# Two decay blocks of a gated recurrence: narrow stationary operands and plain copies in place of full-width products and predicated merges

## The chip, the cores and the metric

The kernel runs on one core of one Trainium2 chip. TensorE (PE) multiplies matrices: it holds a stationary operand, loaded by a weight load (PEld in the profile), and streams a moving operand past it into PSUM. VectorE (DVE), ScalarE (ACT) and GpSimd (POOL) work on tiles in SBUF; SyncE (SP) issues most of the DMA transfers. Each engine executes its own queue in order and waits for others by semaphores. The metric is the time of one execution on the device in microseconds (us), given as the median of several runs.

## The reference, cut to what matters

Two layers, each of a half-step SwiGLU FFN, a mixer and a second half-step FFN, over 512 tokens of width 1024. The mixer has three groups of heads side by side: four of stick-breaking attention (A), four of dilated attention (B) and four of a gated recurrence, HGRN2 (C), with 128 keys and 128 values a head. The change is in the recurrence:

```python
def step(state, xs):
    qb, kb, vb, gb = xs
    diff = gb[:, :, :, None, :] - gb[:, :, None, :, :]
    decay = jnp.where(causal, jnp.exp(jnp.where(causal, diff, 0.0)), 0.0)
    scores = jnp.einsum('bhtd,bhsd,bhtsd->bhts', qb, kb, decay)
    o = jnp.einsum('bhts,bhsv->bhtv', scores, vb) + jnp.einsum('bhtd,bhdv->bhtv', qb * jnp.exp(gb), state)
```

Here `gb` is the running sum of the logarithm of the forget gate. A score of a query t and an earlier key s is a sum over the 128 channels of q, k and a decay that depends on t, s and the channel.

## The kernel before

All of it works on tiles with 128 partitions. Projections and FFNs split both operands into a high and a low fp32r part and take three products (`triple`); the names in the profile are `wt` for the split weights, `h` and `hs` for activations, `m` and `a` for the two pools of PSUM banks (two and six), `u` for the general slots of SBUF, `k` for slots of attention keys, `x` for the residual. Nearly every instruction is recorded through a helper and has the line L113.

**The recurrence.** `hgrn(h)` treats one head, with chunks of 128 tokens (four, `NT`) instead of the reference's 64. Within a chunk, scores are built in the tile `st`, keys on partitions and queries along the free axis, by halving: at the level of block m (`LEVELS` = 64, 32, 16, 8, 4, 2, 1) the second half of every stretch of 2m tokens looks at its first half. With the decay measured from the boundary between the halves, one factor belongs to the keys and one to the queries, and a plain matrix product gives the scores.

- `decay` has POOL subtract the boundary's running sum, two operations a level; ACT takes the exponential; DVE multiplies the first halves by k and the second halves by q. The result is the tile `e`.
- `level` multiplies, for each of the four chunks, all 128 tokens of `e` as stationary columns by the 64 tokens of the second halves as moving columns, in fp32: 128 x 64 results, of which only the (first half, second half) pairs of the same stretch count.
- `merge` copies those into `st` under a mask, with one predicated copy on DVE (`copy_predicated`, mask `level_mask`).
- `chain` runs the seven levels of a head in order. Before it, `st` is set to 0 and the diagonal is merged; after it come the state across chunks, the product with the values, a norm and a gate.

**What sets the order.** The program is written out ahead of time by a planner. Pieces of work are generators that yield a `Step` with its engine and the tiles that it needs; `Flow.run` always advances the one that can start earliest by the planner's clocks. `Flow.cost` prices each instruction, and `to_hi` chooses among engines for a copy by the same clocks. So a changed cost or a changed instruction moves other work of the stage. In a mixer the main stream does the projections; four lanes take the tasks `c0,c1,a0,a1,a2,a3,c2,c3,b0,b1,b2,b3` beside it. Heads c0 and c1 run about 440 to 480 us from the start, c2 and c3 in 560 to 632, the dilated heads until about 680. At the end, the main stream's work is the output projection (`out_ac`, tiles `m<-u,wt` of 512 columns), whose last part (`out_b`) has to wait for the dilated heads; `attend` makes a dilated head's output from its weights, which are transposed (`a<-ident,u`), cast on ACT and subtracted on DVE first. The second layer's mixer, about 1476 to 1716 us, repeats this.

Of the kernel before, what the change touches and what calls it, by code (L numbers as in the profile page):

```python
# [17 lines left out]
P = 128  # L18
# [6 lines left out]
NT = S // P  # L25
# [198 lines left out]
class Flow:  # L224
# [15 lines left out]
    def cost(self, eng, op, out, ins):  # L240
        n = out.free_size()
        if eng == "PE":
            if op == "transpose":
                return 0.109
            if ins[0].dtype == F32R:
                return max(0.112, 0.0133 + n / 2400.0)
            return 2 * max(0.112, n / 1200.0)
        psum = any(a.space == bass.MemoryType.PSUM for a in [out, *ins])
        column = any(a.free_size() == 1 for a in ins)
        if eng == "ACT":  # L250
            return 0.18 + n * 0.00085 + 0.05 * column
        if eng == "DVE":
            if op == "tensor_reduce":
                n = ins[0].free_size()
            fast = op in ("tensor_copy", "tensor_scalar") and not psum
            return (0.2 if fast else 0.15) + n * (0.00053 if fast else 0.00108)
        if eng == "POOL":
            return 0.1 + n * (0.0011 if op == "tensor_scalar" else 0.0022)
        return 0.0
# [88 lines left out]
def trunk(ctx, tc, x, c, w_mod, b_mod, f1g, f1u, f1d, w_in, w_out, qng, kng, hng, lbl, f2g, f2u, f2d, cf, out):  # L348
    nc = tc.nc
    F = Flow()  # L350
    V, A, G, T, Q, Q2 = (Engine(F, e, n) for e, n in (
        (nc.vector, "DVE"), (nc.scalar, "ACT"), (nc.gpsimd, "POOL"), (nc.tensor, "PE"), (nc.sync, "SP"),
        (nc.gpsimd, "SP")))

    def space(name, bufs, **kw):
        return ctx.enter_context(tc.tile_pool(name=name, bufs=bufs, **kw))
# [9 lines left out]
    B = Pool(F, space("psa", 6, space=PS), "a", [P, S], 6)  # L366
# [555 lines left out]
    def next_weight():  # L922
        if not weights:
            yield lambda: bool(weights)
        return weights.popleft()
# [407 lines left out]
    def to_hi(out_, in_, engines=("ACT", "DVE", "POOL")):  # L1333
        n = out_.free_size()
        psum = in_.space == PS
        c = {"ACT": 0.1 + n * 0.00083, "DVE": 0.07 + n * (0.00104 if psum else 0.00052), "POOL": 0.1 + n * 0.0011}
        es = [e for e in engines if not (psum and e == "POOL")]
        e = min(es, key=lambda z: max(F.clk[z], max(F.ready.get(n, 0.0) for n in F.keys(in_))) + c[z])
        if e == "ACT":
            A.copy(out_, in_)  # L1340
        elif e == "DVE":
            V.tensor_copy(out_, in_)
        else:
            G.tensor_scalar(out_, in_, 1.0, 0.0, ALU.mult, ALU.add)

    def mixer(phase, l, hs):
# [147 lines left out]
        def blocks(t, m):  # L1494
            return t.rearrange("p (b w) -> p b w", w=2 * m)

        def hgrn(h):
# [8 lines left out]
            st = U.get()  # L1506
# [11 lines left out]
            def level(idx, e):  # L1518

                m = LEVELS[idx]  # L1520
                ps = B.get()
                for t in range(NT):
                    tt = slice(t * P, (t + 1) * P)
                    T.matmul(ps[:, t * 64:(t + 1) * 64].rearrange("p (b w) -> p b w", w=m), e[:, tt],
                             blocks(e[:, tt], m)[:, :, m:], start=True, stop=True)
                return ps

            def merge(idx, ps):
                m = LEVELS[idx]
                mask = level_mask[:, idx * 64:(idx + 1) * 64].rearrange("p (o b w) -> p o b w", o=1, w=m)  # L1530
                V.copy_predicated(
                    st.rearrange("p (t b w) -> p t b w", t=NT, w=2 * m)[:, :, :, m:],
                    mask.to_broadcast([P, NT, 64 // m, m]),
                    ps[:, :256].rearrange("p (t b w) -> p t b w", t=NT, w=m))
                B.put(ps)

            def chain(which):
                for j, idx in enumerate(which):
                    if j == 0:
                        yield Step("POOL", gc, need=((U, 1),))  # L1540
                        decay(idx)
                    if j + 1 < len(which):
                        yield Step("POOL", need=((U, 1),))
                        decay(which[j + 1])
                    e = es[idx]
                    yield Step("ACT", e)
                    A.activation(e, e, AF.Exp)
                    m = LEVELS[idx]
                    eb = blocks(e, m)
                    yield Step("DVE", e)  # L1550
                    V.tensor_mul(eb[:, :, :m], eb[:, :, :m], blocks(k, m)[:, :, :m])
                    V.tensor_mul(eb[:, :, m:], eb[:, :, m:], blocks(q, m)[:, :, m:])
                    yield Step("PE", e, need=((B, 1),))
                    ps = level(idx, e)
                    U.put(e)
                    yield Step("DVE", ps)
                    merge(idx, ps)

            yield Step("PE", k, q, need=((B, 1),))
            ps = B.get()  # L1560
# [58 lines left out]
            o, sq = qe, U.get()  # L1619
# [236 lines left out]
        for name in PROJ.split(",")[2:]:  # L1856
            kind, p = name[0], int(name[1]) if name[1].isdigit() else 0
# [32 lines left out]
        for d in range(0, ND - 2, 2):  # L1890
            w = yield from next_weight()
# [8 lines left out]
        w = yield from next_weight()  # L1900
# [3 lines left out]
        for t, cs in enumerate(HALVES):  # L1904
            for n, d in enumerate(order[t]):
                pool = (M, B)[n % 2]
                yield Step("PE", need=((pool, 1),))
                ps = pool.get()
# [65 lines left out]
```

## Time and profile before

| | |
|---|---|
| runs | 2100.08, 2101.84, 2103.24 us; median 2101.84 |
| profiled execution | 2105.25 us, span of its instructions 2103.5 us |
| mean granted TensorE clock | 0.992 of full speed |
| level matmuls `a<-u` 128x64 | 448 records (224 matmuls in two passes), 56.0 us busy |
| predicated copies of the levels | 56, 28.7 us busy on DVE |
| POOL's operations of 128x256, the levels' 112 subtractions among them | 162, 136.5 us busy |

A row of the timeline gives the start, the length, the engine, the line, the operation, the tiles written and read, the shape, the count of merged instructions, and in brackets the idle time before them with what ended it. A row of a group has the count, the busy time and mean length of one in ns, and the idle time before. The length of a matmul's record reaches past the start of the next one, since they are pipelined; the spacing of starts is what a matmul costs in a stream. An fp32 matmul has two records, an fp32r one a single record.

### The profile page before, as it was taken

The page shows a single profiled execution, that of the slowest core. Times are in us where ns is not written, and L with a number is a line of the kernel's source. Part 1 is how long each engine was busy: PE and PEld are TensorE (multiplying, and loading weights), DVE is VectorE, ACT ScalarE, POOL GpSimd, SP SyncE. Part 2 cuts the span into 40 slices and gives each one's busy share as a digit, 9 for nine tenths or more (in the row PEclk, how much of TensorE's full clock was granted, in tenths as well). Part 3 has the DMA queues.
Part 4 walks back from the last instruction along what each step waited for, and adds up shares of the span by engine and source line. Part 5 has one row for each costly group of instructions (what it writes and reads, how often), then busy time and mean ns, then how long its engine had stood idle before and what let it go on. Part 6 is the DMA issues. An engine that isn't in the chain of part 4 may idle for free.

```text
span 2103.5 us, 31674 instructions
## 1 busy us (share of the span) xinstructions
PE 2055.7 (98%) x12560; PEld 1839.9 (87%) x12560; DVE 1533.8 (73%) x2411; ACT 980.1 (47%) x1628; POOL 192.1 (9%) x236
## 2 busy tenths in 40 slices
PE   7999999999999999999999999999999999999999
PEld 6888888998988987989898898989888888889897
DVE  6887777787688776867686887767876779657463
ACT  5523434556664542534354252436485645335241
POOL 0000000150240100000000000002314101000000
PEclk8999999999999999999999999999999999999999
DMA  9375566211203244354614636442111142533221
GB/s 329 121 232 183 166 200 220 80 42 41 71 31 103 78 144 156 121 181 140 198 53 131 220 121 220 155 146 81 41 40 52 34 134 65 172 109 120 81 81 40
DMA packets 210564, 259.40 MB, mean 123 GB/s; under 512 B 8896, under 2 KB 192084, under 8 KB 210416
## 3 DMA queue, kind: packets, MB, share of 16 engines
q1 hardware_dynamic: 210160, 257.30, 37.9%
q8 instruction: 98, 1.61, 0.3%
q14 instruction: 50, 0.41, 0.1%
q0 software_dynamic: 256, 0.08, 0.0%
HBM read 255.25 MB, written 2.10 MB: 122 GB/s over the span
## 4 chain that ended last, share of the span: by engine, by line
PE 91%; DVE 5%; ACT 1%; DMA 1%; issue 1%; SPq 0%; ACTq 0%; DVEq 0%
PE m L113 56%; PE a L113 35%; DVE u L113 2%; DVE wt L113 1%; ACT u L113 1%; DMA u<-in_w_mod_dram 1%; DVE h L113 1%; DVE x L113 1%; ACT wt L113 0%; DMA w<-in_ffn_w_gate_dram 0%; DVE acc L113 0%; DVE k L113 0%; DVE c L113 0%; SPq L113 0%; ACT h L113 0%
## 5 line engine op out<-in xcount | busy, mean ns | idle before, releaser
L113 PE MATMUL m<-h,wt 128*128 128x512 f32 (+1 forms) x2940 | 579.6, 348 | 12.8 <-DVE h L113 5.5
L113 DVE TENSOR_TENSOR wt<-w,wt 128x1024 fp32r<-128x1024 f32 (+1 forms) x440 | 504.9, 1153 | 112.2 <-ACT wt L113 101.3
L113 PE MATMUL m<-u,wt 128*128 128x512 f32 (+1 forms) x2712 | 574.5, 370 | 10.0 <-DVE x L113 5.1
L113 ACT CAST wt<-w 128x1024 fp32r<-128x1024 f32 (+1 forms) x440 | 423.8, 980 | 338.5 <-PE m L113 147.7
L113 PEld LDWEIGHTS m<-u,wt 128*128 128x128 f32 x2712 | 469.8, 190 | 94.2 <-DVE x L113 8.3
L113 PEld LDWEIGHTS m<-h,wt 128*128 128x128 f32 x2940 | 465.4, 190 | 80.0 <-DVE h L113 9.1
L113 PE MATMUL a<-h,wt 128*128 128x256 f32 (+1 forms) x2172 | 372.1, 327 | 0.0
L113 PEld LDWEIGHTS a<-h,wt 128*128 128x128 f32 x2172 | 325.7, 191 | 33.7
L113 DVE TENSOR_TENSOR u<-u 128x256 f32<-128x256 f32 (+4 forms) x428 | 248.5, 599 | 40.2 <-ACT u L113 33.6
L113 POOL TENSOR_TENSOR u<-u 128x256 f32<-128x256 f32 x162 | 136.5, 863 | 1315.2 <-ACT u L113 1228.1
L113 PE MATMUL a<-hs,wt 128*128 128x256 f32 x1656 | 213.7, 283 | 0.0
L113 PEld LDWEIGHTS a<-hs,wt 128*128 128x128 f32 x1656 | 205.3, 192 | 0.0
L113 DVE SCALAR_TENSOR_TENSOR x<-m,mod,x 128x512 f32<-128x512 f32 (+1 forms) x136 | 90.8, 670 | 123.0 <-PE m L113 122.7
L113 ACT ACTIVATE u<-u 128x512 f32<-128x512 f32 (+2 forms) x264 | 143.2, 568 | 47.7 <-POOL u L113 29.4
L113 DVE SCALAR_TENSOR_TENSOR acc<-w,sc_c,acc 128x1024 f32<-128x1024 f32 x112 | 143.5, 1282 | 2.0
L113 DVE TENSOR_TENSOR w<-w 128x512 f32<-128x512 f32 x184 | 126.9, 690 | 4.7
L113 PEld LDWEIGHTS a<-u 128*128 128x128 f32 x864 | 115.2, 191 | 15.1 <-DVE u L113 3.3
L113 ACT CAST u<-u 128x512 fp32r<-128x512 f32 x98 | 60.7, 620 | 132.0 <-DVE u L113 124.1
L113 PE MATMUL a<-u 128*128 128x64 f32 (+4 forms) x864 | 117.4, 283 | 4.1 <-DVE u L113 3.0
L113 DVE TENSOR_TENSOR u<-u,a 128x256 f32<-128x256 f32 (+1 forms) x88 | 47.9, 546 | 83.3 <-PE a L113 83.3
L113 ACT COPY u<-a 128x256 f32<-128x256 f32 (+2 forms) x131 | 51.5, 393 | 112.1 <-PE a L113 111.2
L113 PE MATMUL m<-wt,h 128*128 128x256 f32 x768 | 100.9, 292 | 2.0 <-DVE u L113 2.0
(145 smaller groups left out, 1423.6 us busy)
## 6 DMA issues: line engine op xcount, KB each, us to landing
w<-in_w_mod_dram SPq DMA_DIRECT2D x128, 512.0 KB, 4.5
w<-in_ffn_w_gate_dram SPq DMA_DIRECT2D x88, 512.0 KB, 4.7
w<-in_ffn_w_up_dram SPq DMA_DIRECT2D x88, 512.0 KB, 4.8
w<-in_ffn_w_down_dram SPq DMA_DIRECT2D x80, 512.0 KB, 4.6
w<-in_w_in_dram SPq DMA_DIRECT2D x56, 512.0 KB, 4.4
u<-in_w_mod_dram SPq DMA_DIRECT2D x32, 256.0 KB, 6.2
w<-in_w_out_dram SPq DMA_DIRECT2D x24, 256.0 KB, 3.3
w<-in_ffn_w_down_dram SPq DMA_DIRECT2D x16, 256.0 KB, 4.8
```

The source lines that it names most:

```text
L113: ins = fn(*args, **kw)
```

## The change

For the blocks of 64 and 32, `level` now makes one matmul for each stretch of 2m tokens, with only the m keys of its first half as stationary columns and the m queries of its second half as moving columns. For block 64 that is one matmul for each chunk, 64 x 64 in place of 128 x 64; for block 32 two for each chunk, 32 x 32. Each result lies on the partitions of its keys. Since all results count, `merge` copies them with `to_hi` (ACT or DVE), one copy for block 64 and two for block 32, instead of one predicated copy each. The planner's price of an fp32 matmul falls with the number of output partitions. The other blocks are as before.

```diff
-            return 2 * max(0.112, n / 1200.0)
+            return 2 * max(0.112 * out.shape[0] / P, n / 1200.0)
...
                 m = LEVELS[idx]
                 ps = B.get()
+                if m >= 32:
+
+                    for t in range(NT):
+                        for b in range(0, P, 2 * m):
+                            o = t * P + b
+                            T.matmul(ps[b:b + m, t * 64 + b // 2:t * 64 + b // 2 + m], e[:, o:o + m],
+                                     e[:, o + m:o + 2 * m], start=True, stop=True)
+                    return ps
...
             def merge(idx, ps):
                 m = LEVELS[idx]
+                if m >= 32:
+                    for b in range(0, P, 2 * m):
+                        r = slice(b, b + m)
+                        to_hi(st[r].rearrange("p (t w) -> p t w", t=NT)[:, :, b + m:b + 2 * m],
+                              ps[r, :256].rearrange("p (t w) -> p t w", t=NT)[:, :, b // 2:b // 2 + m], ("ACT", "DVE"))
+                    B.put(ps)
+                    return
```

In the built program, PE has 32 matmuls of 64x64 and 64 of 32x32 in place of 64 of 128x64. All 24 copies stand on ACT, 8 of 64x4x64 and 16 of 32x4x32; 16 predicated copies are gone from DVE. Six conversions of 128x512 move from ACT and DVE to POOL.

PE at the first levels of the first layer, before (`a<-u` are the levels of heads 0 and 1 in turn, `m<-h,wt` the projections between them):

```order
L113 MATMUL m<-h,wt 128x512 x9
L113 MATMUL a<-u 128x64 x4
L113 MATMUL m<-h,wt 128x512 x3
L113 MATMUL a<-u 128x64 x4
L113 MATMUL m<-h,wt 128x512 x3
L113 MATMUL a<-u 128x64 x4
L113 MATMUL m<-h,wt 128x512 x3
L113 MATMUL a<-u 128x64 x4
```

The same place after the change:

```order
L113 MATMUL m<-h,wt 128x512 x9
L113 MATMUL a<-u 64x64 x4
L113 MATMUL m<-h,wt 128x512 x6
L113 MATMUL a<-u 64x64 x4
L113 MATMUL m<-h,wt 128x512 x6
L113 MATMUL a<-u 32x32 x8
L113 MATMUL m<-h,wt 128x512 x6
L113 MATMUL a<-u 32x32 x8
```

Between two touched levels stand six projection matmuls now instead of three; every touched level has plain matmuls on both sides.

ACT at the same levels, before the change nothing but the exponentials of the levels (`ACTIVATE u<-u 128x512`) and other work; now:

```order
L113 ACTIVATE u<-u 128x512 x2
L113 COPY u<-a 64x4x64
L113 ACTIVATE u<-u 128x512
L113 COPY u<-a 64x4x64
L113 ACTIVATE u<-u 128x512
L113 COPY u<-a 32x4x32 x2
```

The copies that wait for PE stand between the exponentials, and casts of weights follow later in the queue.

PE at the end of the first mixer, before: the transposes of the last dilated head (`a<-ident,u`), its attention (`a<-u` of 512 to 128 columns) and the output projection (`m<-u,wt`):

```order
L113 MATMUL a<-ident,u 128x128 x4
L113 MATMUL m<-u,wt 128x512 x6
L113 MATMUL a<-ident,u 128x128 x2
L113 MATMUL m<-u,wt 128x512 x3
L113 MATMUL a<-ident,u 128x128 x4
L113 MATMUL m<-u,wt 128x512 x12
L113 MATMUL a<-u 128x512 x3
L113 MATMUL a<-u 128x384 x3
```

The same place after the change:

```order
L113 MATMUL a<-k,u 128x128 x3
L113 MATMUL m<-u,wt 128x512 x18
L113 MATMUL a<-ident,u 128x128 x10
L113 MATMUL a<-u 128x512 x3
L113 MATMUL a<-u 128x384 x3
```

No output matmul stands among or behind the transposes any more (21 did), and the attention follows the transposes at once. The second layer has the same rows there. At the start of this part, the first output matmuls follow nine score matmuls (`a<-k,u 128x512 x9`) where six stood before.

## The prediction

> **What bounds the kernel now.** The page comes first: its span, the busy times, and the chain of work that ended last.
>
> ```profile
> span 2103.5 us, 31674 instructions
> PE 2055.7 (98%) x12560; PEld 1839.9 (87%) x12560; DVE 1533.8 (73%) x2411; ACT 980.1 (47%) x1628; POOL 192.1 (9%) x236
> PE 91%; DVE 5%; ACT 1%; DMA 1%; issue 1%; SPq 0%; ACTq 0%; DVEq 0%
> ```
>
> PE (TensorE) is busy for 98% of the span and holds 91% of the chain, so an edit counts by the PE time that it takes away or adds, and by the waits that it opens in front of PE. Since a busy PE is not PE at its peak, I then look at how close its instructions start. The change sits in the two mixers, so the busy times by stage come next (columns: length, then PE, PEld, DVE, ACT, POOL with counts, the granted clock, DMA).
>
> ```profile
> 440.00:480.00 40.00, 39.97 (x262) 35.77 (x262) 33.30 (x61) 18.13 (x34) 18.15 (x24) 1.00 0.09 28
> 560.00:632.00 72.00, 69.11 (x463) 61.40 (x463) 55.05 (x93) 45.10 (x81) 27.22 (x35) 1.00 0.11 34
> 632.00:680.00 48.00, 45.46 (x245) 38.20 (x243) 39.87 (x115) 24.01 (x56) 0.00 (x0) 1.00 0.28 89
> ```
>
> The first stretch holds the levels of heads 0 and 1, the second those of heads 2 and 3, the third the end of the mixer. PE is full in the first and idle for 2.9 and 2.5 us in the others; DVE is at 76 to 83%, ACT at 45 to 63%. What PE waited for from 440 to 700 us (in total, times, longest):
>
> ```profile
> PE m L113 <- DVE u L113: 3.1, 3, 1.2
> PE a L113 <- DVE u L113: 1.5, 1, 1.5
> ```
>
> So most of what PE waits for there is DVE, at the end of the stage and not at the levels.
>
> **A level now.** PE's order of time in the first chain, and a run of seven plain matmuls for their spacing:
>
> ```profile
> 445.48 1.00 PE L113 MATMUL a<-u 128*128 128x64 f32 x8
> 446.29 0.94 PE L113 MATMUL m<-h,wt 128*128 128x512 f32 x3
> 447.07 1.00 PE L113 MATMUL a<-u 128*128 128x64 f32 x8
> 56.47 1.75 PE L113 MATMUL a<-h,wt 128*128 128x512 f32 x7
> L113 PE MATMUL m<-h,wt 128*128 128x512 f32 x1632 | 403.1, 397 | 2.0 <-ACT h L113 1.7 <-DVE h L113 0.3
> ```
>
> A level is four fp32 matmuls, eight records: two passes each, each with a weight load. From level to level it is 1.59 us. The seven matmuls start (1.75 - 0.39) / 6 = 0.227 us apart, so the three between take 0.68, and a level 0.91 us, or 0.114 us a pass. Sixteen levels are touched (two levels, eight heads over both layers): 14.6 us of PE.
>
> **What a narrower pass costs.** No pass of this trace has fewer than 128 stationary columns, so I bound it. Above: the price does not depend on the columns and stays 0.114. Below: the streaming of the moving columns, from an fp32 matmul with 512 of them:
>
> ```profile
> 607.59 1.02 PE L113 MATMUL a<-u,kept 128*128 128x512 f32 x2
> L113 PE MATMUL a<-u,kept 128*128 128x512 f32 x16 | 8.2, 592 | 0.0
> ```
>
> Its two passes start 1.02 - 0.59 = 0.43 us apart, 0.84 ns a column: 0.054 us for 64 columns and 0.027 for 32. Block 64 keeps eight passes: 0.43 to 0.91 us. Block 32 goes from eight to sixteen: 0.43 to 1.82 us. I take 0.057 for both, half the price for half the columns, and no less for a quarter: that is the middle, in ratio, of 0.027 and 0.114. So block 64 has 0.46 us of passes, block 32 has 0.91.
>
> The Trainium skill, "TensorE: Matmul & The Clock Gate", section "LDWEIGHTS (loading the stationary operand)", lets a weight load take its columns divided by 1.2 ns: 107, 53 and 27 ns for 128, 64 and 32. The 0.114 us above agrees with the first; no run here shows the others. By that rule alone, block 32 would stay at its lower bound.
>
> **What a change of array shape costs.** In the built program all matmuls of before have the tile 128x128, but for two transposes of few rows (32x128); the new ones have 128x64 and 128x32. One of the two transposes, of tpar, runs between plain matmuls; the transpose of tb comes from the same helper, with the tile 128x128.
>
> ```profile
> 58.15 0.23 PE L113 MATMUL a<-ident,tpar 14*128 14x14 f32 x1
> 58.31 1.43 PE L113 MATMUL m<-h,wt 128*128 128x512 f32 x5
> 58.15 0.14 PEld L113 LDWEIGHTS a<-ident,tpar 14*128 14x128 f32 x1 [0.35 <-issue]
> 96.04 1.24 PE L113 MATMUL a<-h,wt 128*128 128x256 f32 x9
> 97.12 0.23 PE L113 MATMUL a<-ident,tb 72*128 72x72 f32 x1
> 97.15 0.60 PE L113 MATMUL a<-h,wt 128*128 128x256 f32 x3
> 97.02 0.14 PEld L113 LDWEIGHTS a<-ident,tb 72*128 72x128 f32 x1
> ```
>
> Ahead of tpar the last matmul starts at 57.83 (56.47 + 6 x 0.227), the second one behind it at 58.67 (the end 59.74, less 0.39 and three spacings): 0.84 us, or 0.38 beyond two spacings. For tb the same runs from 97.00 to 97.35: 0.11 beyond two spacings of 0.12. The weight load of tpar came late for "issue", which names no engine. I read the difference, 0.27 us, as the way into another shape and back; the lower bound for columns instead of rows is nothing. All sixteen levels have plain matmuls on both sides, so each pays it: 4.3 us.
>
> The Trainium skill, "TensorEngine Tiling (Array Packing)", section "Key Properties", speaks against the change with the same mechanism: a change of tiling mode drains the array. The late load at 58.15 agrees; without the rule and the row the sum below would be 4.3 us lower.
>
> **Sum on PE.** Block 64: 0.27 + 0.46 - 0.91 = -0.18 us. Block 32: 0.27 + 0.91 - 0.91 = +0.27. A head +0.09, eight heads +0.7 us. Bounds: -7.7 us (no switch, lower prices: 2 x -0.48 x 8) and +11.6 (0.27 + 0.27 + 0.91 = 1.45 a head).
>
> **Merges.** Sixteen predicated copies go from DVE; 24 plain copies come, all on ACT by the new order: 8 of 256 elements and 16 of 128.
>
> ```profile
> L113 DVE COPY_PREDICATED u<-level_mask,a 128x256 f32<-128x256 uint8 x56 | 28.7, 524 | 10.2 <-PE a L113 10.2
> L113 ACT COPY u<-a 128x256 f32<-128x256 f32 x115 | 42.8, 372 | 94.0 <-PE a L113 93.1
> L113 ACT COPY u<-a 128x512 f32<-128x512 f32 x10 | 5.8, 583 | 12.5 <-PE a L113 12.5
> ```
>
> DVE loses 16 x 0.52 = 8.4 us. ACT gains 8 x 0.37 + 16 x 0.27 (the two rows continued to 128 elements) = 7.3 us. Both lie beside PE, so I count nothing. A copy now waits for PE in ACT's queue, with exponentials and weight casts behind it; ACT has at least a third of these stretches free. Were that cover gone, a wait would be about a copy, 0.4 us, a level. On the other side, DVE's relief can at most end PE's waits for it, 4.6 us in this layer. The planner also hands six conversions from ACT and DVE to POOL, which is 9% busy; SP's transfers keep their order.
>
> **The order at the mixer's end.** The planner's new costs move other work. For the last dilated head, the order shows ten transposes in a row and the attention matmuls at once behind them, where twelve matmuls stood between. Before:
>
> ```profile
> 673.39 0.60 PE L113 MATMUL a<-ident,u 128*128 128x128 f32 x4
> 673.75 3.00 PE L113 MATMUL m<-u,wt 128*128 128x512 f32 x12
> 674.03 0.59 ACT L113 CAST u<-a 128x512 fp32r<-128x512 f32 x1 [0.71 <-PE a L113]
> 674.65 0.69 DVE L113 TENSOR_TENSOR u<-a,u 128x512 fp32r<-128x512 f32 x1 [0.87 <-ACT u L113]
> 676.58 2.02 PE L113 MATMUL a<-u 128*128 128x512 f32 x12
> 672.95 0.37 ACT L113 CAST u<-a 128x256 fp32r<-128x256 f32 x1 [1.05 <-PE a L113]
> 634.48 0.96 PE L113 MATMUL m<-u,wt 128*128 128x512 f32 x3 [1.21 <-DVE u L113]
> ```
>
> The twelve covered the cast and the subtraction: the attention at 676.58 waited for nothing. Now the first cast starts 0.64 us after the first transpose, three casts take 0.59 + 0.37 + 0.59, the last subtraction 0.69, with hand-overs 3.0 us; ten transposes (0.11 each, as tb's) take 1.1. PE stands for 1.9 us. Against that, the first output group now follows nine score matmuls instead of six, so 0.7 of the 1.2 us of wait at 634.48 goes. Net 1.2 us a layer, 2.4 us in all; bounds nothing (the work moved ahead fills other waits) and 3.8.
>
> **Total:** +0.7 + 2.4 = +3.1 us. The profiled execution took 2105.25 us (span 2103.5), 3.4 above the median; I put the difference on the median, 2101.84: **2104.9 us**. A measurement of this kernel can tell 0.2%, 4.2 us, from no change.
>
> **Rivals.**
> *A, narrow passes are no cheaper.* PE pays 0.114 for each of block 32's sixteen passes: +11.6 + 2.4 = 2115.9 us. For it: all passes seen, transposes included, start 0.11 us apart or more, as a fixed price would have it; against it: all have 128 columns. It decides early: with the rest as forecast, 0.066 us for block 32's 128 passes makes +4.2.
> *B, no price for the shape.* tpar's gap came from something else, narrow passes stream at their bound, and the end loses nothing: -7.7, 2094.1 us. Against it stands tb, the same helper without the gap.
> *C, the load's columns alone.* Switches at 0.27 and lower bounds for the passes: (0.27 + 0.43 - 0.91) x 2 x 8 = -3.4, with the end's 2.4 a little under before: 2100.8 us. The page's rule for weight loads gives this.
> *D, DVE was the limit.* With 8.4 us off DVE, two thirds of PE's waits for it (4.6 us here, as much taken for the other mixer) go, -6.1, and with them the end's new wait: 0.7 - 6.1 = -5.4, 2096.4 us. Against it: the waits lie behind chains of single operations, not behind a full queue.
>
> **How the numbers follow.** Forecast 0.38, of which 0.14 beyond +4.2; A in all its degrees from 0.066 on 0.22; C 0.20, of which 0.01 beyond -4.2; B 0.14, of which 0.03 within; D 0.06. Faster 0.01 + 0.11 + 0.06 = 0.18; slower 0.14 + 0.22 = 0.36; same 0.46. The range goes over the bounds of the unknown costs, from B to A: 2094 to 2116; the forecast alone has 2102 to 2107.
>
> **What would show it.** Level to level in the new first chain: six matmuls (1.36 us) and 0.73 us for block 64, 1.18 for block 32. Steps between weight loads inside a group give the narrow pass; the time from the last plain matmul to the first narrow load, and back, gives the switch. The twelve attention matmuls behind the ten transposes should carry a wait of about 1.9 us in each layer. The forecast is wrong if block 32 takes much under 0.8 or over 1.4 us, or if PE's waits from 560 to 700 us do not grow.

## The result, and the profile after

| | before | after |
|---|---|---|
| median of the runs | 2101.32 us (4 runs, 2100.08 to 2103.24) | 2123.24 us (4 runs, 2118.61 to 2127.56) |
| ratio to before | | 1.0100, 95% interval 1.0085 to 1.0115 |
| profiled execution | 2105.25 us, span 2103.5 | 2127.56 us, span 2125.8 |

The change makes the kernel slower by 1%, some 22 us by the medians. The four runs after the change fall into two groups, 2118.6 and 2119.4 us and 2127.1 and 2127.6 us, so no run lies at the median, and the profile is of the later group. Span and busy times of the changed kernel:

```profile
span 2125.8 us, 31767 instructions
PE 2062.4 (97%) x12624; PEld 1838.3 (86%) x12624; DVE 1526.7 (72%) x2395; ACT 985.8 (46%) x1646; POOL 200.4 (9%) x242
```

PE is busy for 7 us more, though 64 full-width matmuls became 96 narrower ones, and idle for 16 us more. (The busy time holds matmuls that ran at half clock in this execution; a second profile, of after_again below, with less of that, has PE busy for 2054.3 us.) The touched levels come first. PE's timeline of the first chain, and its weight loads there:

```profile
445.25 0.68 PE L113 MATMUL a<-u 128*64 128x64 f32 x8
445.86 1.66 PE L113 MATMUL m<-h,wt 128*128 128x512 f32 x6
447.45 0.68 PE L113 MATMUL a<-u 128*64 128x64 f32 x8
...
449.66 0.45 PE L113 MATMUL a<-u 128*32 128x32 f32 x16
450.03 1.67 PE L113 MATMUL m<-h,wt 128*128 128x512 f32 x6
451.63 0.45 PE L113 MATMUL a<-u 128*32 128x32 f32 x16
```

```profile
445.25 0.54 PEld L113 LDWEIGHTS a<-u 128*64 128x64 f32 x8 [0.36 <-issue]
...
449.66 0.33 PEld L113 LDWEIGHTS a<-u 128*32 128x32 f32 x16 [0.37 <-issue]
```

Grouped by shape, over the stretch from 440 to 640 us:

```profile
L113 PEld LDWEIGHTS a<-u 128*64 128x64 f32 x32 | 2.2, 137 | 1.4 <-issue 1.4
L113 PEld LDWEIGHTS a<-u 128*32 128x32 f32 x64 | 1.3, 112 | 1.5 <-issue 0.7 <-ACT u L113 0.7
```

Level to level is 2.20 us for block 64 and 1.97 for block 32. Less six matmuls (1.36 us) that leaves **0.84 and 0.61 us a level**, against 0.91 before. One load's length taken off, eight loads of 64 columns start (0.54 - 0.137) / 7 = 0.058 us apart, sixteen of 32 columns (0.33 - 0.112) / 15 = 0.015. Eight passes of 0.058 and sixteen of 0.015 leave 0.38 us a level, the same for both blocks; I put this remainder down to the change of shape. So the levels themselves got cheaper, by 0.07 + 0.30 = 0.37 us a head, 3.0 us in all. The loss lies elsewhere.

What PE waits for in total (times, longest), after and then before:

```profile
PE a L113 <- DVE u L113: 10.3, 4, 3.0
PE m L113 <- DVE k L113: 7.7, 2, 3.8
```

```profile
PE m L113 <- DVE x L113: 7.9, 11, 2.0
PE m L113 <- DVE h L113: 5.5, 13, 1.0
PE m L113 <- DVE u L113: 5.4, 6, 1.2
```

A wait for `k` of 3.8 us in each mixer is new. PE's waits in the first mixer of the changed kernel, from its timeline:

```profile
491.20 11.53 PE L113 MATMUL m<-wt,h 128*128 128x256 f32 x72 [3.84 <-DVE k L113]
...
631.74 1.38 PE L113 MATMUL a<-u 128*128 128x128 f32 x10 [2.95 <-DVE u L113]
...
681.30 1.25 PE L113 MATMUL a<-ident,u 128*128 128x128 f32 x10
683.39 0.50 PE L113 MATMUL a<-u 128*128 128x512 f32 x1 [0.84 <-ACT u L113]
686.08 3.36 PE L113 MATMUL a<-u 128*128 128x512 f32 x11 [2.18 <-DVE u L113]
690.10 2.16 PE L113 MATMUL m<-u,wt 128*128 128x256 f32 x6 [0.67 <-ACT u L113]
```

The first row is where nothing was expected. DVE's queue ahead of it, ACT's cast of the same keys, and then the same subtraction on DVE before:

```profile
483.65 0.75 DVE L113 SCALAR_TENSOR_TENSOR u<-u,par 128x512 f32<-128x512 f32 x1 [5.10 <-ACT u L113]
484.44 0.69 DVE L113 TENSOR_TENSOR u<-u 128x512 f32<-128x512 f32 x1
485.22 0.75 DVE L113 SCALAR_TENSOR_TENSOR u<-u,par 128x512 f32<-128x512 f32 x1
486.01 1.58 DVE L113 TENSOR_TENSOR u<-u 128x512 f32<-128x512 f32 x2
487.51 1.63 DVE L113 TENSOR_TENSOR wt<-w,wt 128x1024 fp32r<-128x1024 f32 x1
489.06 0.68 DVE L113 TENSOR_TENSOR u<-u 128x512 fp32r<-128x512 f32 x1
489.67 1.38 DVE L113 TENSOR_TENSOR k<-m,k 64x512 fp32r<-64x512 f32 x2
```

```profile
485.09 1.17 ACT L113 CAST k<-m 64x512 fp32r<-64x512 f32 x2
```

```profile
486.22 1.39 DVE L113 TENSOR_TENSOR k<-m,k 64x512 fp32r<-64x512 f32 x2 [1.07 <-ACT k L113]
```

The keys lie in one of the two banks `m`; until their low part is subtracted out of it, PE has no bank for the next projection. ACT's cast is done at 486.26. Before, the subtraction stood next in DVE's queue and waited for the cast itself. Now heads 0 and 1 end together, and the norms and gates of both, with a split of weights between, stand ahead of it: it starts 3.4 us later, and PE stands still for 3.84 us. DVE is not short of time: ahead of the first of these rows it was idle for 5.10 us.

The second row, 2.95 us at 631.74, lies at the end of heads 2 and 3. Before, the corresponding row had half the wait, 9 us earlier:

```profile
622.62 1.38 PE L113 MATMUL a<-u 128*128 128x128 f32 x10 [1.48 <-DVE u L113]
```

The stretch from 480 to 560 us, before and after (PE, PEld, DVE, ACT, POOL, then the granted clock):

```profile
480.00:560.00 80.00, 79.88 (x476) 71.03 (x476) 56.79 (x96) 56.02 (x97) 14.44 (x19) 1.00 0.20 63
```

```profile
480.00:560.00 80.00, 76.04 (x435) 67.67 (x434) 51.35 (x87) 52.31 (x93) 10.93 (x14) 0.96 0.17 53
```

PE loses 3.84 us to the wait, and the clock, 0.96 over 80 us, takes another 3.2: behind the wait it is granted at half speed for 6.8 us. Seven microseconds are gone in one stretch that was full before.

Lateness against before, at the same instruction of DVE in both traces (weight splits and residual updates counted from the start), in us, for `after` and for five of the runs below:

```
before at (us)      432    497    685    832   1425   1575   1721   2002
after              -0.3    5.7   11.0   10.7   10.7   16.4   21.0   22.3
after_again        -1.1    3.7    5.5    5.2    5.2   10.6   11.8   13.1
after_keys_first   -1.0    0.8    6.1    8.3    8.4    9.8   13.0   14.3
after_true_c01     -0.5   -0.8    3.1    2.8    2.7    2.2    5.4    7.8
after_true_c23      0.2    6.1    4.8    3.5    3.5    7.9    4.5    6.1
after_true_price   -1.5   -2.0   -4.8   -6.2   -6.2   -6.8   -8.6   -7.1
```

From 832 to 1425, in the FFNs, nothing changes. In `after` each mixer loses some 6 us up to the keys and 5 more to its end. In after_again, the same kernel in an execution of the earlier group, the two parts are 4.8 and 1.8 us in the first mixer, 5.4 and 1.2 in the second: the early part stays, the late one is mostly the difference between the groups.

### The profile page after: what moved, and what is told of

It is laid out like the page before. It is cut to its first block, busy times and chain, and to the rows that moved or that the text cites. A ratio compares the mean times of both kernels' runs of the same rounds, so it can differ in the third digit from the quotient of the medians.

```text
span 2125.8 us, 31767 instructions
## 1 busy us (share of the span) xinstructions
PE 2062.4 (97%) x12624; PEld 1838.3 (86%) x12624; DVE 1526.7 (72%) x2395; ACT 985.8 (46%) x1646; POOL 200.4 (9%) x242
## 4 chain that ended last, share of the span: by engine, by line
PE 91%; DVE 5%; ACT 1%; issue 1%; POOL 1%; DMA 1%; SPq 0%; POOLq 0%; DVEq 0%; ACTq 0%
PE m L113 56%; PE a L113 35%; DVE u L113 2%; DVE wt L113 1%; DVE acc L113 1%; ACT u L113 1%; POOL u L113 1%; DVE x L113 0%; DVE h L113 0%; DVE k L113 0%; DMA w<-in_ffn_w_up_dram 0%; ACT wt L113 0%; DMA u<-in_x_dram 0%; ACT h L113 0%; SPq L113 0%
## 5 line engine op out<-in xcount | busy, mean ns | idle before, releaser
L113 DVE TENSOR_TENSOR u<-u 128x256 f32<-128x256 f32 (+3 forms) x428 | 242.7, 584 | 53.3 <-ACT u L113 46.8
L113 PEld LDWEIGHTS a<-u 128*128 128x128 f32 (+2 forms) x928 | 107.7, 179 | 30.3 <-DVE u L113 11.3
L113 PE MATMUL a<-u 128*128 128x64 f32 (+6 forms) x928 | 114.0, 273 | 12.2 <-DVE u L113 10.3
L113 ACT COPY u<-a 128x256 f32<-128x256 f32 (+4 forms) x155 | 58.6, 378 | 141.5 <-PE a L113 140.3
L113 PE MATMUL m<-wt,h 128*128 128x256 f32 x768 | 107.2, 300 | 8.9 <-DVE k L113 7.7
L113 PEld LDWEIGHTS m<-wt,h 128*128 128x128 f32 x768 | 101.4, 204 | 13.6 <-issue 11.1
```

What stands on the lines that cost most here:

```text
L113: ins = fn(*args, **kw)
```

## The experiments

The theories: (1) the new order, made from new prices, makes the loss; (2) the narrow matmuls or (3) the copies on ACT do. "Plan" is the planner's order. All ratios are to the kernel before, measured beside each run.

| run | median us (runs) | ratio, 95% interval |
|---|---|---|
| new_work_old_plan | 2104.17 (11) | 1.0003, 0.9994 to 1.0011 |
| old_work_new_plan | 2123.62 (4) | 1.0098, 1.0084 to 1.0112 |
| copies_only_old_plan | 2105.09 (11) | 1.0007, 0.9999 to 1.0016 |
| narrow_dve_old_plan | 2105.30 (11) | 1.0010, 1.0001 to 1.0019 |
| halves_apart_old_plan | 2105.39 (1) | one run |
| after_true_price | 2098.15 (9) | 0.9978, 0.9968 to 0.9988 |
| true_price_again | 2098.63 (11) | 0.9980, 0.9971 to 0.9989 |
| old_work_true_plan | 2105.67 (11) | 1.0011, 1.0002 to 1.0019 |
| after_near_price | 2110.56 (6) | 1.0032, 1.0020 to 1.0044 |
| after_old_price | 2118.78 (5) | 1.0078, 1.0066 to 1.0091 |
| after_cast_act | 2120.22 (4) | 1.0091, 1.0075 to 1.0106 |
| after_keys_first | 2119.00 (5) | 1.0071, 1.0058 to 1.0085 |
| after_true_c01 | 2112.88 (5) | 1.0038, 1.0026 to 1.0050 |
| after_true_c23 | 2110.89 (5) | 1.0033, 1.0021 to 1.0045 |
| after_warm_end | 2127.62 (4) | 1.0125, 1.0111 to 1.0138 |
| after_warm_last | 2127.44 (4) | 1.0117, 1.0104 to 1.0130 |
| after_warm_b1 | 2117.89 (5) | 1.0073, 1.0059 to 1.0086 |
| after_again | 2119.16 (6) | 1.0082, 1.0069 to 1.0095 |

### Is it the work or its order?

**new_work_old_plan** charges the planner with the old instructions and issues the new ones:

```diff
+                    F.account("PE", "matmul", o_, [e[:, tt], r_])
+                    if m in (64, 32):
+                        for b in range(0, P, 2 * m):
+                            T.real.matmul(ps[b:b + m, ...], e[:, o:o + m], e[:, o + m:o + 2 * m], start=True, stop=True)
```

> The changed kernel's instructions (narrow matmuls for blocks 64 and 32, copies on ACT) in the order of before: the planner is charged with the old matmuls and the old predicated merges. Theory 1, the order made the loss: the trace of the changed kernel has 0.82 us for a block 64 and 0.59 us for a block 32 against 0.91, so 8 x (0.09 + 0.32) = 3.3 us under before, about 2098 us, with PE's waits and half-clock stretches as before. Theory 2, the narrow shapes or the copies on ACT made it (late copies in ACT's queue, a clock gate that sees less activity): 10 to 22 us over before, with the waits of 3.8 us for DVE k and the long half-clock stretches at 490 and 685 us still there.

**old_work_new_plan** is the reverse: 128-column levels and predicated copies at the places of the changed kernel.

> The instructions of before (full-width matmuls, predicated merges on DVE) in the order of the changed kernel: the planner is charged with the new matmuls and copies. Theory 1 (order): about 22 + 3 = 25 us over before, near 2126 us, with the wait of about 3.8 us for DVE k at 487 us in each mixer. Theory 2 (shapes or copies): within 3 us of before, no such wait.

Old instructions in the new order lose all of it (with the same rows: 3.84 us for `k`, 2.95 for `u`), new ones in the old order lose nothing. Theory 1 holds; 2 and 3 fall. But the 3.0 us by which the levels are cheaper do not show either, against what was expected. PE's and POOL's timelines of new_work_old_plan:

```profile
449.07 0.96 PE L113 MATMUL m<-h,wt 128*128 128x512 f32 x3
450.59 0.45 PE L1530 MATMUL a<-u 128*32 128x32 f32 x16 [0.55 <-DVE u L113]
```

```profile
448.00 2.96 POOL L113 TENSOR_TENSOR u<-u 128x256 f32<-128x256 f32 x4 [0.29 <-issue]
```

A level's two subtractions take POOL 1.5 us, back to back in this chain. With three projection matmuls between the levels, as the old order has it, PE was just slow enough for that; faster levels reach the next one before its operand is there, and the gain becomes a wait. PE's list has four such waits at the touched levels, 2.2 us in all; that the rest of the 3.0 us goes the same way is not shown.

### The parts, in the order of before

**copies_only_old_plan**: full-width matmuls, plain copies on ACT. **narrow_dve_old_plan**: narrow matmuls, the plain copies on DVE. **halves_apart_old_plan**: as new_work_old_plan, but block 32 issues its four first halves, then the four second ones:

```diff
-                    for t in range(NT):
-                        for b in range(0, P, 2 * m):
+                    for b in range(0, P, 2 * m):
+                        for t in range(NT):
```

> Full-width matmuls as before, but the counting parts of blocks 64 and 32 are copied by ACT instead of merged by DVE, in the order of before. If the copies lie beside PE, within 1 us of before. If DVE was the limit of the mixer's end, up to 5 us under it. If copies on ACT hold up the exponentials behind them, some us over it.

> Narrow matmuls as in the changed kernel, plain copies on DVE, in the order of before. If PE's own saving is what counts under the old order: 3.3 us under before, the same as with the copies on ACT. If it needs DVE's relief too: less than half of that.

> As new_work_old_plan, but block 32 makes the four chunks of its first halves (array columns 0 to 31) and then the four of its second halves (columns 64 to 95), where they alternated. If the halves run side by side only when they alternate, the passes of one half start about 0.027 to 0.031 us apart instead of 0.0157, and a level of block 32 takes about 0.2 us longer. If the spacing of 0.0157 is the price of a 32-column pass, nothing changes there.

Neither the copies nor the engine that makes them moves the time by more than 0.2%, and the 3.3 us expected of the narrow matmuls do not come here either. The weight loads of block 32 in halves_apart_old_plan:

```profile
449.49 0.48 PEld L1533 LDWEIGHTS a<-u 128*32 128x32 f32 x16 [0.36 <-ACT u L1549]
```

Sixteen loads take 0.48 us where they took 0.33. In the single records, loads of one half start 0.031 us apart; when the halves alternate, a load for array columns 64 to 95 follows one for columns 0 to 31 by 0.007, and the pairs are 0.031 apart. So two column groups run side by side, and 0.015 is half of 0.031.

### The price that the planner is told

The change prices a level of either block at 4 x 0.112 = 8 x 0.056 = 0.448 us; it takes 0.84 and 0.61. **after_true_price** states about what single records give (4 x 0.205, 8 x 0.074):

```diff
-            return 2 * max(0.112 * out.shape[0] / P, n / 1200.0)
+            return {64: 0.205, 32: 0.074}.get(out.shape[0], 2 * max(0.112, n / 1200.0))
```

**after_old_price** keeps the price of before (0.224 for any matmul), **after_near_price** says 0.19 and 0.09, and **old_work_true_plan** puts the old instructions in the order of after_true_price.

> The changed kernel with the planner's price for the narrow matmuls set to what the trace of the changed kernel shows, the way into the other array shape and back included: 0.205 us each for the four of a block 64 (0.82 us) and 0.074 each for the eight of a block 32 (0.59 us). The order that comes out has the twelve output matmuls between the last transposes and the last attention again. If the too low price made the bad order: no 3.8 us wait for DVE k, no 2 us wait at the end, 2098 to 2102 us. If any new order loses (the old one was a lucky one): 2106 us or more.

> The version with measured prices once more, on this call's chip. 2096 to 2101 us, a ratio of 0.997 to 0.999 to the kernel before.

> The changed kernel with the planner's old price, 0.224 us for an fp32 matmul of any width: about right for a block 64 (0.90 against 0.82 us), three times too high for a block 32 (1.79 against 0.59). Its order has the last four transposes directly before the last attention in each mixer. The theory of the order: a wait of about 1.6 us there and a half-clock stretch behind it, no 3.8 us wait for DVE k, in all 4 to 10 us over before, well under the changed kernel. If the copies and narrow matmuls make the loss whatever the order: near 2123 us.

> The changed instructions with prices close to the measured ones: 0.19 a matmul for block 64 and 0.09 for block 32 instead of 0.205 and 0.074 (levels of 0.76 and 0.72 instead of 0.82 and 0.59). If a right price makes a good order, this is within 3 us of 2098. If the order's quality is a matter of chance and 2098 was a lucky draw, it can lie anywhere from 2098 to 2122; then the lesson is the order, not the price.

> The instructions of before (128-column levels, predicated copies on DVE) in the order that the planner makes for the changed ones at measured prices. It tells apart what made after_true_price 4.6 us faster than before. If the narrow products give it: each level pair costs PE 0.41 us more, eight heads 3.3 us, so about 2101.5 us, 3 us over after_true_price. If the order alone gives it: within 1 us of 2098. If the narrow products pay only in that order through DVE or ACT as well: over 2102.5.

With measured prices the same instructions are 0.2% faster than the kernel before, twice. The page of that run:

```profile
span 2096.4 us, 31775 instructions
PE 2049.4 (98%) x12624; PEld 1827.3 (87%) x12624; DVE 1529.6 (73%) x2407; ACT 983.4 (47%) x1640; POOL 189.7 (9%) x236
```

The wait for `k` is gone, and the twelve output matmuls stand before the last attention again. Prices of 0.82 and 0.59 us a level give -4 us against before; 0.76 and 0.72 give +8; 0.448 for both gives +22 and +15 in two measurements; 0.896 and 1.79 give +16. For after_old_price I had expected 4 to 10 us of loss: the direction was right, the size not. after_near_price was expected within 3 us of after_true_price if a right price makes a good order; it is 12 us over it, with the wait for `k` at 2.3 us in each mixer. Four draws show no law: the price that is furthest off is not clearly the worst, and the step of 12 us between two prices that differ by 7 and 22% says that the order jumps. That the measured price came out best may be luck. old_work_true_plan shows that it is not the order alone: the old instructions in that order are 0.1% slower than before. Of the 7 us between the two, 3.0 are the levels; the rest is not settled (one trace of old_work_true_plan has PE waiting for the chain for 1.0 us in the first mixer and half clock at the mixer's end, which after_true_price's does not have but true_price_again's has).

### Which places of the order

**after_cast_act**: POOL has more conversions by the new order; here those at the end of a recurrent head stay on ACT or DVE.

```diff
-            to_hi(hi, o)
+            eng = to_hi(hi, o, do=False)
+            F.account(eng, ...)
+            (V if eng == "DVE" else A).real...(hi, o)
```

> The changed kernel with its order kept, but the conversions that the planner gives POOL at the end of each recurrent head run on ACT (two of POOL's rows of 1.0 to 1.2 us in place of ACT's 0.62). If POOL's slow conversions ahead of DVE's subtractions make the 3.8 us wait for DVE k, it shrinks to 2 us or less and the time by 3 us or more. If DVE's queue is late anyway because both heads end together, the wait stays over 3 us and the time within 2 us of the changed kernel.

The wait for `k` stays at 3.80 us: POOL is not its cause. **after_keys_first** moves one row in each mixer, the keys' subtraction, to where DVE would issue it right behind head 1's product:

```diff
+            if src.space == PS:
+                for j, t in enumerate(tiles):
+                    o = slice(64 * j, 64 * j + 64)
+                    V.real.tensor_sub(t[o, S:], src[o], t[o, :S])
             for j, t in enumerate(tiles):
...
-                V.tensor_sub(t[o, S:], src[o], t[o, :S])
+                if src.space == PS:
+                    F.account("DVE", "tensor_sub", t[o, S:], [src[o], t[o, :S]])
+                else:
+                    V.tensor_sub(t[o, S:], src[o], t[o, :S])
```

> The changed kernel, with one row moved in each mixer: the two subtractions of the keys, for which PE waits 3.84 us at 491 us, stand in DVE's queue right behind the product for head c1 instead of five instructions later; everything else as in the changed kernel. Theory (the wait is DVE's queue, and PE's loss there carries to the end): the subtractions run at about 486.3 to 487.7, PE's wait falls from 3.84 to under 1.2 us in both layers, the half-clock stretch of 6.8 us behind it goes or shrinks (it cost about 3.4 us of work), and 3 to 6 us a mixer go: 2111 to 2117 us. Rival (the place is cushioned: the end of the mixer depends on the chain of the dilated heads): PE's wait moves to a later place and the time stays within 3 us of 2122.

PE's and DVE's timelines of that run:

```profile
487.17 3.10 PE L113 MATMUL m<-wt,h 128*128 128x256 f32 x24 [0.47 <-DVE k L1413]
491.79 6.02 PE L113 MATMUL m<-wt,h 128*128 128x256 f32 x48 [1.52 <-DVE u L113]
```

```profile
485.63 1.39 DVE L1413 TENSOR_TENSOR k<-m,k 64x512 fp32r<-64x512 f32 x2 [1.16 <-ACT k L113]
```

3.84 us of wait became 0.47 and a new 1.52 behind what was pushed back. Lateness at 497 falls from 5.7 to 0.8 us, and over both stretches of the keys it grows by 1.8 + 1.4 us, against 6.0 + 5.7 in `after` and 4.8 + 5.4 in after_again. So most of the early loss is this one row. But the median, 2119.0, missed the expected 2111 to 2117 us: the ratio falls by 0.3 of 1.0% against the first measurement, by 0.1 against after_again, within the intervals. The trace shows what hides the gain: behind the waits at the mixers' ends, which stay, its execution has half clock for 10.2 us in the first mixer, as `after` has and after_again has not. Against the profiled execution of `after` it is 8.0 us faster. Four of its five runs (2118.8 to 2119.6 us) have a mean clock of 0.988 to 0.990, the fifth (2114.5 us) 0.993; in the changed kernel the later group has 0.986 to 0.987, the earlier one 0.991 to 0.993. So its runs seem to split as well, and what the row is worth in a median stays open.

**after_true_c01** and **after_true_c23** set the measured price for heads 0 and 1 alone, or for 2 and 3 alone:

```diff
+            if self.true_price and out.shape[0] in (32, 64):
+                return {64: 0.205, 32: 0.074}[out.shape[0]]
...
+                F.true_price = h in (0, 1)
```

> The changed kernel with the measured prices (0.205 and 0.074 a matmul) for the blocks of 64 and 32 of heads 0 and 1 alone; heads 2 and 3 keep the change's prices. In its order the early part of the mixer is that of after_true_price, and the end is that of the changed kernel: eighteen output matmuls, ten transposes in a row, the last attention at once behind them. It tells how much of the loss of 21 us is made early (the wait for the keys' subtraction, lateness 5.7 us a mixer at 497 us) and how much late. If the two add up as the marker times of the changed kernel say (early 5.7, later 5 a mixer): 2108 to 2113 us, with the waits of 0.84 and 2.18 us at the end unchanged. If the early loss is only moved (the end waits longer by what comes earlier): over 2117. If the end costs nothing where the stage comes to it in time: under 2105.

> The reverse: measured prices for heads 2 and 3 alone. The order up to about 560 us is that of the changed kernel, with the wait of 3.8 us for the keys' subtraction; the end is that of before, with twelve output matmuls between the last transposes and the last attention. If early and late loss add up: the early one stays, 5 to 6 us a mixer over after_true_price, 2108 to 2113 us. If the end is what costs (the early loss would be made up behind a slack end): under 2105. If the early wait costs everything: over 2117.

Early and late loss add up. The wait rows of PE's list, of after_true_c01 and then of after_true_c23:

```profile
PE a L113 <- DVE u L113: 11.0, 6, 3.0
```

```profile
PE m L113 <- DVE k L113: 7.7, 2, 3.8
```

The first has the end of `after` and no wait for `k`; the second the reverse. Over after_true_price they lie 14.7 and 12.7 us; together 27, where `after` itself lies 21 to 25 above it. So the loss against after_true_price is about half early and half late.

### The half clock behind a wait

**after_warm_end** was to fill PE's last wait with nine extra matmuls:

```diff
             ps = B.get()
+            if name == "b" and h == 3:
+                f_ = got[vname, 0][0]
+                for _ in range(9):
+                    T.real.matmul(ps, f_[:, :P], f_[:, :S], start=True, stop=True)
```

> The changed kernel with nine more matmuls (fp32r, 128x512, 2.0 us) on operands that are ready, ahead of the attention of the last dilated head, into the bank that it then overwrites; they run while PE would wait 0.8 and 2.2 us. If the idle PE lets the clock fall: the half-clock stretch of 10.2 us behind this wait shrinks to 7 us or less in each mixer and the time falls by 3 us or more over both. If the half clock there has another cause, the time stays or grows by up to 1 us.

**after_warm_last** has h == 2 instead, **after_again** is the changed kernel once more.

> The changed kernel with nine extra matmuls (512 columns, 2.0 us, result overwritten) right ahead of the attention that waits last in the mixer; after_warm_end had put them ahead of the one before it, where PE did not wait, so there they were plain extra work of 2 x 2.1 us. They fill PE's wait of 0.84 + 2.18 us. If the half clock behind that wait (10.2 us in each mixer) costs time: it goes or falls to 3.4 us, and 2 to 6 us over both mixers go, 2117 to 2121. If it costs nothing, because the norm and the residual behind the output set the pace there: within 2 us of 2123. If the extra matmuls delay the attention: up to 2125.

> The changed kernel once more, unchanged, so that the other runs of this call are compared with it on one chip. 2119 to 2127 us.

Both missed: head 3 and head 2 are not the last to end; head 1 is. The matmuls stood where PE did not wait, as plain extra work of 2 x 2.0 us. Both runs are some 4 us over the first median of the changed kernel and 8 over after_again's; in their traces the last wait is still there, with half clock of 3.4 us behind it. after_again brought the clue: of the ten runs of the changed kernel seven lie at 2118.4 to 2119.9 us and three at 2126.8 to 2127.6. The profile of `after` is one of the three, that of after_again one of the seven. Their stretch at the end of the first mixer, `after` first (the clock is the third number from the right):

```profile
680.00:700.00 20.00, 16.16 (x90) 14.65 (x89) 8.87 (x15) 5.10 (x11) 2.21 (x3) 0.74 0.33 109
```

```profile
680.00:700.00 20.00, 15.97 (x123) 14.99 (x122) 10.05 (x20) 5.13 (x12) 2.21 (x3) 1.00 0.24 79
```

The same program, with the same waits of 0.84 and 2.18 us, gets 10.2 us of half clock in one execution and none in the other, in both mixers alike. **after_warm_b1** puts the matmuls at head 1, between the ten transposes and the last attention.

> The changed kernel with the nine extra matmuls at the place where PE does wait: between the ten transposes and the last attention (head b1). after_warm_end and after_warm_last, meant for this place, had put them ahead of other dilated heads' attention, where they were 2 x 2.0 us of plain extra work. They should fill 2.0 of the wait of 0.84 + 2.18 us, which then is about 1 us. The runs of the changed kernel fall into two groups, 2119 and 2127 us; in the traces the first has no half clock behind this wait, the second 10.2 us of it, which takes 3.4 us at each mixer's end. If that half clock is the second group's 8 us: all runs at 2117 to 2121. If not: both groups stay, or 2123 and more.

```profile
680.72 2.31 PE L1676 MATMUL a<-u 128*128 128x512 f32 x9
682.87 0.39 PE L113 MATMUL a<-u 128*128 128x512 f32 x1
684.48 1.90 PE L113 MATMUL a<-u 128*128 128x512 f32 x11 [1.22 <-DVE u L113]
```

The eleven matmuls take 1.90 us where they took 3.36 at half clock in `after`, and all five runs lie at 2116.8 to 2120.9. That fits: between the two traces of the changed kernel, the mixers' two ends make 3.5 and 3.4 of the 9.2 us of lateness. It is not proof: after_again has 1.89 us for the eleven matmuls without the filling, and with three of ten runs in the later group, five in a row would miss it one time in six.

## Why the prediction was wrong, step by step

- **PE bounds the kernel:** right; PE is busy for 97% of the span after the change.
- **Block 64, -0.18 us a level:** measured -0.07. The pass was right (0.058 for 0.057); what is left of the level, put down to the change of shape, is 0.38, not 0.27.
- **Block 32, +0.27 us a level:** measured -0.30. The pass was the mis-sized term: 0.015 for 0.057. I had refused less for a quarter of the columns than for half. The lower bound of 0.027 was itself too high, since the two halves run side by side. The rule on weight loads that the prediction weighed (the Trainium skill, "TensorE: Matmul & The Clock Gate", section "LDWEIGHTS (loading the stationary operand)": columns divided by 1.2 ns) gives 0.053 and 0.027; the trace has 0.058 and, for one half alone, 0.031.
- **Levels in all, +0.7 us:** -3.0. In the old order the time does not show it, in part at least because the levels wait for POOL's chain. In the order of after_true_price the new instructions are faster than the old ones.
- **Merges at nothing:** right in the order of before (copies_only_old_plan). DVE's predicated copies fell by 6.6 us, ACT's plain ones cost 7.0; neither is seen in the time.
- **The order at the mixer's end, +1.2 us a layer:** the place and the mechanism were right, the size was not. From the attention before (668.78 to 674.91) to the first output matmul (679.27 to 690.10), lateness grows by 4.7 us; in after_again, without half clock there, by 3.2. The wait in front of the first output group, of which 0.7 us was to go, did go. Two causes were left out. I let the last subtraction follow its cast at once, though two weight splits and a residual update, 3 us, stood before it in DVE's queue (wait 3.0 us with ACT's 0.84, for 1.9). And behind the wait there can be half clock (3.36 us for the eleven matmuls in `after`, 1.89 in after_again). DVE and ACT at that place, after:

```profile
681.48 2.35 DVE L113 TENSOR_TENSOR wt<-w,wt 128x1024 fp32r<-128x1024 f32 x2
683.75 0.74 DVE L113 SCALAR_TENSOR_TENSOR x<-m,mod,x 128x512 f32<-128x512 f32 x1
684.41 1.61 DVE L113 TENSOR_TENSOR u<-a,u 128x512 fp32r<-128x512 f32 x3
```

```profile
681.99 1.35 ACT L113 CAST u<-a 128x512 fp32r<-128x512 f32 x3 [0.91 <-PE a L113]
```

  The three casts end at 683.34, the first subtraction starts at 684.41.
- **The step that failed: the order was priced at one place.** I counted "+2.4" for the mixer's end and nothing for the rest, so the stretch from 480 to 560 us, full in the trace of before, came out at no loss. There DVE's queue changed as well: the keys' subtraction fell behind five instructions of heads 0 and 1. By the table, lateness grows by 6.0 and 5.7 us there in `after`, half of its 22.3 us, and by 4.8 and 5.4 in after_again, most of its 13.1; with the subtraction alone moved back (after_keys_first), by 1.8 and 1.4. The wait of 2.95 us at 631.74, at the end of heads 2 and 3, was not foreseen either; by markers of the same kind, lateness grows by 2.4 us from 560 to 632 in `after` and falls by 0.8 until 662. What I wrote of heads 0 and 1 was that ACT has a third of the stretch free; a free third says nothing of who stands in front of whom when PE holds two banks and needs one back.
- **The rivals:** A (whose sum is 2115.8, not 2115.9) ended on the right side for a wrong reason (narrow passes are cheaper). B's and C's cheap passes are real, but without the loss in the order. D falls with copies_only_old_plan. Of the two stated signs of error, the one on block 32, "much under 0.8" us, came true with 0.61. The other, on PE's waits from 560 to 700 us, did not: they grew. The stretch ahead of it, where the wait for `k` is, had no sign at all.

## What to carry to other kernels

When a price in a planner changes, treat it as a new order everywhere: compare the queues of every engine in each stretch that was full before, and look above all for the instruction that frees a PSUM bank, since one that falls behind five others on a half-idle engine stops PE. Measure what a new instruction takes and give the planner that; here the same instructions are 1% slower or 0.2% faster by this alone. A nearly right price is no safeguard (+8 us here), so compare several orders by their time. And where executions of one kernel fall into groups, compare traces of the same group. To tell work from order, charge the planner with one and issue the other.

## What the hardware showed that was not expected

- Matmuls of 32 stationary columns in two groups of array columns run side by side: sixteen loads in 0.33 us alternating, in 0.48 us one group after the other.
- Beyond its passes, a level of narrow matmuls between full-width ones costs 0.38 us, for 64 and for 32 columns alike. The first narrow weight load starts 0.36 us after the load before it has ended. No run separates the change of shape from other causes.
- Half clock after a wait of PE of 2 to 4 us comes in stretches of 3.4, 6.8 or 10.2 us, or not at all, for one program: behind the wait of 3.84 us 6.8 us in `after` and 3.4 in after_again (first mixer), behind the last one 10.2 and none. `before` has 3.4 us of it at 682 us, behind waits of 0.67 and 0.91 us, so it also came behind shorter ones. By the two executions of the changed kernel it is worth 3.4 us at a mixer's end: lateness grows by 3.7 us from 662 to 685 us in `after` and by 0.4 in after_again.
